# A two-layer trunk on one core: the sums of activation quarters made on POOL, and the matmuls that first write the sums' banks set behind the first product

## The chip, the core and the metric

The kernel runs on one core of a Trainium2 chip. The core's engines are TensorE (PE, with its weight loads PEld), VectorE (DVE), ScalarE (ACT), GpSimd (POOL) and SyncE (SP), which here only issues DMAs. The engines run side by side, each through its own list of instructions in order, and wait for each other through semaphores. The metric is the device time of one execution in microseconds (us).

## The reference

Two layers, each of three parts; every part has a normalisation before and after and is added to x.

```python
for l in range(DEPTH):
    h = hybrid_mixer(rmsnorm(x, pre_mix_g[l]), ...)
    x = x + rmsnorm(h, post_mix_g[l])
    h = memory_cross_attention(rmsnorm(x, pre_mem_g[l]), mem, ...)
    x = x + rmsnorm(h, post_mem_g[l])
    h = conv_ffn(rmsnorm(x, pre_ffn_g[l]), w_up[l], fconv_w[l], fconv_b[l], w_down[l])
    x = x + rmsnorm(h, post_ffn_g[l])

def conv_ffn(h, w_up, conv_w, conv_b, w_down):
    u = causal_dwconv(h @ w_up, conv_w, conv_b)
    a, g = jnp.split(u, 2, axis=-1)
    return (jax.nn.gelu(g, approximate=True) * a) @ w_down
```

x has 512 tokens of 1024 features; `w_up` is 1024 x 5632, that is 22 pairs of 128 linear and 128 gate columns. The change lies where the part `conv_ffn` of each layer begins.

## The kernel before

**Precision.** A float32 matrix product is made of three matmuls. `split` (L98) writes the rounded value of an operand on ACT (`ACT.copy`, L99: "hi") and the remainder on DVE (`DVE.tensor_sub`, L100: "lo"); `mm3` then adds hi x hi, hi x lo and lo x hi in one PSUM bank.

**Before the up projection.** After cross-attention the class `Tail` handles x in four pieces of 128 tokens, t = 0 to 3. For each piece `pre_norm` (L239) normalises, and `to_feature` (L270) transposes on PE, casts to hi on ACT (L276, tiles `B`), makes lo on DVE (L277, also `B`) and, for this part alone, copies the float32 values to a tile `T` (ACT, L279). With pieces t = 2 and t = 3 `Forms.add` (L299) makes sums and differences of the quarters of the activations (pieces 0 with 2, and 1 with 3), four additions of 128x512 (L308 to L311), each of which needs the one before it, and splits two results of 128x1024 into the tiles `S` (hi on ACT L99, lo on DVE L100): the first can be split after the second addition, the other after the fourth.

**The up projection.** Columns 0 and 1 are made in the plain way by `feat_halves`: four units (linear and gate of each), 24 matmuls of 256 tokens for the first half of each unit, then the same for the second half, which needs pieces 2 and 3. A unit's result is a PSUM bank `pg`; when it is complete, ACT takes the middle tap of the convolution (L1026), DVE the other two (L1031), and gate units then go through the gelu (L1053). From column 2 on, `up_products` makes seven smaller products per column in place of eight (Strassen's scheme in Winograd's form), from sums of weight quarters (POOL, L1101 to L1104, tiles `T`, numbers 1 to 4 of `add_up`) and the sums `S`. Each product is 12 matmuls of 256 tokens. Products 1, 5, 6 and 7 go to banks `pa`; products 2, 3 and 4 are added on top of sums that ACT and DVE have copied into two of four banks `pg` per column (`total(j)`). These four `pg` banks are those in which `feat_halves` made its four units, so each comes free when the taps of that unit are done. Before the first copy into them, in columns 2 and 3 alone, one matmul with `start=True` writes each of the two banks of a column; its values are overwritten.

**What sets the order.** PE's instructions stand in the order of the code, into which waiting tasks such as `pre_norm` are mixed by a clock of estimated times. Up to the end of `feat_halves` the instructions of ACT, DVE and POOL are ordered by the framework's scheduler, which places them by its own estimates; behind that point (`manual_schedule`, in `ffn`) they stand in the order of the code, and so do SP's DMAs within `up_products`. Weight tiles `raw` have two buffers and `rg` two: a load waits until the last reader of its buffer is done. `whi` and `wlo` have five.

The two steps of the prediction lie in `Forms.add` (L308 to L311) and in `first` (L1148). Layers are called 0 and 1, pieces t2 and t3; column 2's weights are tiles `whi`, `wlo` and `T`, column 3's the next ones.

Of the kernel before, what the change touches and what calls it, by code (L numbers as in the profile page):

```python
# [14 lines left out]
ALU = mybir.AluOpType  # L15
# [23 lines left out]
def trunk_kernel(ctx: ExitStack, tc: tile.TileContext, x4, memt, w, gw, gains, mcw, fcw, gb,  # L39
# [3 lines left out]
    ACT, DVE, POOL, PE, SP = nc.scalar, nc.vector, nc.gpsimd, nc.tensor, nc.sync  # L43
# [7 lines left out]
    def nm(s):  # L51
        uid[0] += 1
        return f"{s}_{uid[0]}"
# [4 lines left out]
    def pa():  # L58
        return ps.tile([128, 512], F32, tag="a", name=nm("pa"), bufs=4)
# [38 lines left out]
    def split(src, hi, lo):  # L98
        ACT.copy(hi, src)  # L99
        DVE.tensor_sub(lo, src, hi.bitcast(F32))  # L100
# [3 lines left out]
    def mm(o, lhs, rhs, **kw):  # L104
        n = math.prod(o.shape[1:])
        now[0] += 0.0025 + (max(0.218, n / 600) if rhs.dtype == F32 else max(0.107, n / 2400))
        PE.matmul(o, lhs, rhs, **kw)  # L107
# [5 lines left out]
    def mm3(o, lh, ll, rh, rl, start, stop, **kw):  # L113
        mm(o, lh, rh, start=start, stop=False, **kw)
        mm(o, lh, rl, start=False, stop=False, **kw)
        mm(o, ll, rh, start=False, stop=stop, **kw)
# [164 lines left out]
    class Forms:  # L281
# [19 lines left out]
        def add(self, t, xf):  # L301
            self.xf[t] = xf
            if t < 2:
                return
            self.s = self.s or [self.wide(F32R) for _ in range(4)]
            a, b = self.xf[t - 2], xf
            a11, a12, a21, a22 = a[:, :4], a[:, 4:], b[:, :4], b[:, 4:]
            DVE.tensor_add(a22, a21, a22)  # L308
            DVE.tensor_sub(a21, a11, a21)
            DVE.tensor_sub(a11, a22, a11)  # L310
            DVE.tensor_sub(a12, a12, a11)  # L311
            c = slice(128 * (t - 2), 128 * (t - 2) + 128)
            for i, f in ((0, b), (2, a)):
                split(f, self.s[i][:, :, c], self.s[i + 1][:, :, c])
# [755 lines left out]
    def up_products(l, fp, xn, forms, us, conv_first, conv_rest, gated, gtiles):  # L1070
# [13 lines left out]
        raws, rgs, ts, ws, e1s, p5s = {}, {}, {}, {}, {}, {}  # L1084
# [48 lines left out]
        def total(j):  # L1133
            i = 2 * (j % 2)
            return sums[i], sums[i + 1]

        def product(o, j, i, start=False):
            kind, c0 = {1: ("a", 0), 2: ("a", 512), 5: ("t", 0), 6: ("t", 512), 3: ("b", 0), 7: ("u", 0),
                        4: ("u", 512)}[i]
            hi, lo = ws[j, kind]  # L1140
            for q in range(4):
                c = slice(c0 + 128 * q, c0 + 128 * q + 128)
                rh, rl = act[i](q)
                mm3(o, hi[:, c], lo[:, c], rh, rl, start and q == 0, q == 3, skip_group_check=not start)
                if q % 2:
                    yield

        def first(j):  # L1148
            e1s[j] = pa()[:, left]
            if j < j0 + 2:  # L1150
                for o in total(j):
                    mm(o, ws[j, "a"][0][:, :128], xn[0][:, 0, :], start=True, stop=True)
            yield from product(e1s[j], j, 1, True)

        for j in (j0, j0 + 1):
            load_a(j)
# [3 lines left out]
        for kind in "atu":  # L1160
            high(j0, kind)
            low(j0, kind)
        high(j0, "b")
        yield from first(j0)
        ACT.copy(total(j0)[0][:, left], e1s[j0])
        high(j0 + 1, "a")
        low(j0 + 1, "a")
        ready = []
        for j in range(j0, NF + 1):
# [31 lines left out]
            if j + 1 == NF:  # L1201
                ready.append(down_tile(0))
            else:
                yield from first(j + 1)
# [168 lines left out]
```

## Time and profile before

| | us |
|---|---|
| median of 3 runs | 1577.7 |
| lowest and highest of them | 1573.72, 1581.47 |
| profiled execution | 1576.06 |
| its span, first to last instruction | 1574.3 |

| engine | busy us | share of the span |
|---|---|---|
| PE | 1547.4 | 98% |
| DVE | 1049.2 | 67% |
| ACT | 892.0 | 57% |
| POOL | 326.5 | 21% |

The profile gives each instruction's start and length on its engine, and in brackets the idle time of the engine before it with the instruction that ended it. An instruction that is held up after it was sent shows a longer time, not idle time. A line with x2 or more merges instructions of one kind that follow each other. The granted clock of PE is 0.997 of full speed over the span.

### The profile page before, as it was taken

What the parts mean: (1) busy time and instruction counts of PE and PEld (TensorE: products, weight loads), DVE (VectorE), ACT (ScalarE), POOL (GpSimd) and SP (SyncE); (2) the same over time, 40 slices, a digit from 0 to 9 for tenths busy, and PEclk for the clock granted to TensorE, in tenths of its full rate; (3) what the DMA queues carried; (4) which work ended last, traced back from release to release, by engine and by line L of the source; (5) the groups of instructions that cost most, each with busy time, mean ns of one, the idle gap of its engine ahead of it and who ended that gap; (6) DMA issues with size and microseconds to landing.
All of it is one profiled execution on the core that took longest, in us unless ns stands there. A gap on an engine that the chain in (4) does not pass through costs nothing.

```text
span 1574.3 us, 24497 instructions
## 1 busy us (share of the span) xinstructions
PE 1547.4 (98%) x9480; PEld 1371.0 (87%) x9480; DVE 1049.2 (67%) x1808; ACT 892.0 (57%) x1578; POOL 326.5 (21%) x292
## 2 busy tenths in 40 slices
PE   7999999999999999999999999999999999999998
PEld 5788888998899999988887888889888899999886
DVE  5687646746597777763376886557566977777433
ACT  5677574545466666653257775745445666666321
POOL 0000110100026666600010002101000466663000
PEclk9999999999999999999999999999999999999999
DMA  5421244552242333332333223445411233332331
GB/s 177 129 94 62 92 137 153 155 187 94 68 136 95 108 108 108 108 121 94 108 95 107 94 74 94 137 144 161 161 54 42 96 108 108 108 114 82 127 102 58
DMA packets 55430, 173.13 MB, mean 110 GB/s; under 512 B 6801, under 2 KB 9617, under 8 KB 55314
## 3 DMA queue, kind: packets, MB, share of 16 engines
q1 hardware_dynamic: 55314, 171.57, 33.4%
q8 instruction: 74, 1.21, 0.3%
q14 instruction: 42, 0.34, 0.1%
HBM read 165.22 MB, written 6.33 MB: 109 GB/s over the span
## 4 chain that ended last, share of the span: by engine, by line
PE 82%; DVE 6%; DMA 5%; ACT 3%; issue 2%; POOL 1%; SPq 0%; POOLq 0%; DVEq 0%; ACTq 0%
PE pg L107 51%; PE pa L107 28%; PE pa L111 2%; DMA raw<-in_w_dram 2%; DVE wlo L100 1%; DMA raw<-in_memt_dram 1%; ACT whi L99 1%; DVE xg L256 1%; POOL sm L230 1%; ACT junk L235 1%; DVE x L369 1%; DMA raw<-dk 1%; DVE wlo L1126 1%; DMA raw<-dv 1%; DMA dk<-kf 0%
## 5 line engine op out<-in xcount | busy, mean ns | idle before, releaser
L107 PE MATMUL pg<-B,whi 128*128 128x256 f32 (+1 forms) x1800 | 420.7, 327 | 8.2 <-DVE ql L995 3.9
L100 DVE TENSOR_TENSOR wlo<-raw,whi 128x1024 fp32r<-128x1024 f32 x188 | 230.6, 1228 | 215.7 <-ACT whi L99 213.1
L99 ACT CAST whi<-raw 128x1024 fp32r<-128x1024 f32 x188 | 197.2, 1050 | 217.8 <-PE pg L107 139.7
L107 PEld LDWEIGHTS pg<-B,whi 128*128 128x128 f32 x1800 | 290.8, 189 | 28.3 <-DVE ql L995 4.3
L107 PE MATMUL pg<-whi,B 128*128 128x512 f32 x896 | 297.8, 399 | 0.0
L107 PE MATMUL pg<-B,wlo 128*128 128x256 f32 (+1 forms) x896 | 288.4, 322 | 0.0
L107 PEld LDWEIGHTS pg<-whi,B 128*128 128x128 f32 x896 | 168.6, 188 | 35.1 <-DVE B L100 1.3
L230 POOL TENSOR_TENSOR sm<-sm,mhalf 128x1 f32<-128x1 f32 x56 | 34.3, 612 | 724.2 <-DVE sm L355 548.3
L107 PEld LDWEIGHTS pg<-B,wlo 128*128 128x128 f32 x896 | 168.9, 188 | 13.6
L107 PE MATMUL pg<-wlo,B 128*128 128x512 f32 x448 | 175.3, 391 | 0.6 <-DVE sm L248 0.6
L107 PE MATMUL pa<-S,whi 128*128 128x256 f32 x960 | 175.5, 283 | 0.0
L1031 DVE SCALAR_TENSOR_TENSOR u<-pg,fcw,u 128x511 f32<-128x511 f32 (+1 forms) x176 | 131.3, 747 | 38.2 <-ACT u L1026 35.2
L107 PEld LDWEIGHTS pa<-S,whi 128*128 128x128 f32 x960 | 148.4, 190 | 0.0
L107 PE MATMUL pa<-S,wlo 128*128 128x256 f32 x480 | 135.6, 282 | 0.0
L1126 DVE TENSOR_TENSOR wlo<-T,whi 128x1024 fp32r<-128x1024 f32 x80 | 103.9, 1299 | 9.7 <-ACT whi L1120 9.7
L107 PE MATMUL pa<-whi,S 128*128 128x512 f32 x320 | 105.9, 390 | 0.0
L107 PE MATMUL pg<-whi,S 128*128 128x512 f32 x320 | 105.4, 390 | 0.0
L1120 ACT CAST whi<-T 128x1024 fp32r<-128x1024 f32 x80 | 83.5, 1044 | 32.9 <-PE pg L107 30.8
L1026 ACT ACTIVATE u<-pg,fcw 128x512 f32<-128x512 f32 x88 | 68.5, 779 | 57.2 <-PE pg L107 37.2
L107 PEld LDWEIGHTS pg<-wlo,B 128*128 128x128 f32 x448 | 84.7, 189 | 15.8 <-DVE wlo L100 1.0
L107 PEld LDWEIGHTS pa<-S,wlo 128*128 128x128 f32 x480 | 90.9, 189 | 0.0
L1126 POOL TENSOR_TENSOR b<-rg,b 128x512 fp32r<-128x512 f32 x40 | 51.6, 1290 | 142.7 <-ACT b L1120 142.7
(264 smaller groups left out, 2942.5 us busy)
## 6 DMA issues: line engine op xcount, KB each, us to landing
raw<-in_w_dram SPq DMA_DIRECT2D x228, 512.0 KB, 3.5
rg<-in_w_dram SPq DMA_DIRECT2D x40, 512.0 KB, 3.5
gain<-in_gains_dram SPq DMA_DIRECT2D x11, 512.0 KB, 4.0
raw<-in_memt_dram SPq DMA_DIRECT2D x20, 256.0 KB, 3.0
tb<-tb_d SPq DMA_DIRECT2D x16, 256.0 KB, 3.5
x<-in_x_dram SPq DMA_DIRECT2D x8, 256.0 KB, 5.6
e<-nmu_d SPq DMA_DIRECT2D x8, 256.0 KB, 3.7
dv<-vf SPq DMA_DIRECT2D x8, 256.0 KB, 4.4
```

Of the source, the lines that this page charges most:

```text
L99: ACT.copy(hi, src)
L100: DVE.tensor_sub(lo, src, hi.bitcast(F32))
L107: PE.matmul(o, lhs, rhs, **kw)
L111: PE.transpose(o, src, idn)
L230: POOL.tensor_tensor(r, v, mhalf[:, :1], ALU.pow)
L235: ACT.activation(junk[:, :src.shape[-1]], src, AF.Square, accum_out=s_)
L256: DVE.scalar_tensor_tensor(xg, xt[:, c], r, g[h], ALU.mult, ALU.mult)
L369: DVE.scalar_tensor_tensor(xs[t][:, cc], self.hg[hh, t], r, xs[t][:, cc], ALU.mult, ALU.add)
L1026: ACT.activation(u, acc, AF.Identity, bias=fcw_t[:, m, 3:4], scale=fcw_t[:, m, 2:3])
L1031: DVE.scalar_tensor_tensor(u[:, q:], acc[:, :512 - q], fcw_t[:, m, 2 - q:3 - q], u[:, q:], ALU.mult, ALU.add)
L1120: ACT.copy(ws[j, kind][0], source(j, kind))
L1126: sub(ws[j, kind][1], source(j, kind), ws[j, kind][0].bitcast(F32), ALU.subtract)
```

## The change

The four additions of `Forms.add` move from DVE to POOL, with the same operands. In `first` the one or two matmuls that write the banks of a column's sums for the first time are issued behind the twelve matmuls of product 1 in place of ahead of them.

```diff
             a11, a12, a21, a22 = a[:, :4], a[:, 4:], b[:, :4], b[:, 4:]
-            DVE.tensor_add(a22, a21, a22)
-            DVE.tensor_sub(a21, a11, a21)
-            DVE.tensor_sub(a11, a22, a11)
-            DVE.tensor_sub(a12, a12, a11)
+            POOL.tensor_tensor(a22, a21, a22, ALU.add)
+            POOL.tensor_tensor(a21, a11, a21, ALU.subtract)
+            POOL.tensor_tensor(a11, a22, a11, ALU.subtract)
+            POOL.tensor_tensor(a12, a12, a11, ALU.subtract)
...
         def first(j):
             e1s[j] = pa()[:, left]
+            yield from product(e1s[j], j, 1, True)
             if j < j0 + 2:
                 for o in total(j):
                     mm(o, ws[j, "a"][0][:, :128], xn[0][:, 0, :], start=True, stop=True)
-            yield from product(e1s[j], j, 1, True)
```

Because the scheduler orders ACT, DVE and POOL here, the move of four additions also changes the order of other instructions. On ACT in layer 0, between the end of piece t2 and column 2's first weights (`B`: hi of piece t3; `S_4656`: the split that needs t2's fourth addition; `whi_4695`: hi of the fourth unit of `feat_halves`; `whi_4956`: column 2's):

```order
 L420 COPY kf_4645<-pg_4620 128x256
 L276 CAST B_4157<-pa_4667 128x4x128
+L99 CAST S_4656<-T_4403 128x8x128
+L99 CAST whi_4695<-raw_4693 128x1024
+L279 COPY T_4666<-pa_4667 128x512
 L276 CAST B_4158<-pa_4709 128x4x128
-L99 CAST whi_4695<-raw_4693 128x1024
-L99 CAST S_4656<-T_4403 128x8x128
-L279 COPY T_4666<-pa_4667 128x512
 L1120 CAST whi_4956<-raw_4940 128x1024
 L279 COPY T_4666<-pa_4709 128x512
```

The cast that needs the fourth addition now stands ahead of the cast of the fourth unit's weights, which stood ahead of it before.

On ACT in layer 1, at the same place (`S_12568` and `S_12570`: the two splits of t2; `B_12168` and `B_12169`: hi of piece t3):

```order
 L279 COPY T_12539<-pa_12540 128x512
 L279 COPY T_12539<-pa_12554 128x512
+L99 CAST S_12568<-T_12539 128x8x128
+L99 CAST S_12570<-T_12372 128x8x128
 L276 CAST B_12168<-pa_12617 128x4x128
-L99 CAST S_12568<-T_12539 128x8x128
 L276 CAST B_12169<-pa_12631 128x4x128
-L99 CAST S_12570<-T_12372 128x8x128
 L279 COPY T_12616<-pa_12617 128x512
 L279 COPY T_12616<-pa_12631 128x512
```

Both splits of t2 now stand ahead of both casts of piece t3; before, one cast stood ahead of each split.

On POOL in layer 0 (`T_4563`, `T_4403`: t2's operands; `T_4666`, `T_4491`: t3's; `T_4948`, `T_4949`: column 2's weight sums):

```order
 L230 TENSOR_TENSOR sm_4453<-sm_4451,mhalf 128x1
+L308 TENSOR_TENSOR T_4563<-T_4563 128x512
+L309 TENSOR_TENSOR T_4563<-T_4403,T_4563 128x512
+L310 TENSOR_TENSOR T_4403<-T_4563,T_4403 128x512
+L311 TENSOR_TENSOR T_4403<-T_4403 128x512
+L308 TENSOR_TENSOR T_4666<-T_4666 128x512
 L1101 TENSOR_TENSOR T_4948<-rg_4942,raw_4940 128x512
+L309 TENSOR_TENSOR T_4666<-T_4491,T_4666 128x512
 L1102 TENSOR_TENSOR T_4948<-rg_4942,T_4948 128x512
+L310 TENSOR_TENSOR T_4491<-T_4666,T_4491 128x512
+L311 TENSOR_TENSOR T_4491<-T_4491 128x512
 L1103 TENSOR_TENSOR T_4949<-rg_4942 128x512
```

The additions of t3 and those of column 2's weights now share one list, two of the latter between the former. In layer 1 the list is L1101, L1102, the four additions of t3, L1103, L1104.

## Rows read from the trace of the kernel before

**Rows 1.** The page's part 1: busy us, share of the span, instructions.

```profile
PE 1547.4 (98%) x9480; PEld 1371.0 (87%) x9480; DVE 1049.2 (67%) x1808; ACT 892.0 (57%) x1578; POOL 326.5 (21%) x292
```

**Rows 2.** Waits of PE, whole span: us in total, times, longest us.

```profile
PE pg L107 <- DVE u L1031: 2.8, 2, 2.0
PE pa L107 <- DVE wlo L1126: 2.2, 2, 1.2
```

**Rows 3.** Timeline of DVE, layer 0: start us, length us, then the instruction.

```profile
452.93 1.22 DVE L100 TENSOR_TENSOR wlo<-raw,whi 128x1024 fp32r<-128x1024 f32 x1 [1.00 <-ACT whi L99]
...
455.79 1.22 DVE L100 TENSOR_TENSOR wlo<-raw,whi 128x1024 fp32r<-128x1024 f32 x1 [0.31 <-ACT whi L99]
...
459.87 1.21 DVE L100 TENSOR_TENSOR wlo<-raw,whi 128x1024 fp32r<-128x1024 f32 x1
...
464.87 1.79 DVE L308 TENSOR_TENSOR T<-T 128x512 f32<-128x512 f32 x1
...
476.83 2.97 DVE L1031 SCALAR_TENSOR_TENSOR u<-pg,fcw,u 128x511 f32<-128x511 f32 x4
```

**Rows 4.** Timeline of ACT, layer 0.

```profile
452.79 0.59 ACT L279 COPY T<-pa 128x512 f32<-128x512 f32 x1
...
457.93 1.05 ACT L99 CAST whi<-raw 128x1024 fp32r<-128x1024 f32 x1
459.39 1.05 ACT L99 CAST S<-T 128x1024 fp32r<-128x1024 f32 x1 [0.41 <-DVE T L311]
...
462.86 0.59 ACT L279 COPY T<-pa 128x512 f32<-128x512 f32 x1 [0.99 <-DVE B L277]
...
470.77 0.78 ACT L1026 ACTIVATE u<-pg,fcw 128x512 f32<-128x512 f32 x1
```

**Rows 5.** Timeline of POOL, layer 0.

```profile
462.56 1.30 POOL L1101 TENSOR_TENSOR T<-rg,raw 128x512 f32<-128x512 f32 x1 [14.41 <-DMA rg<-in_w_dram]
463.94 2.17 POOL L1102 TENSOR_TENSOR T<-rg,T 128x512 f32<-128x512 f32 x1
```

**Rows 6.** Timeline of PE, layer 0.

```profile
477.27 0.40 PE L107 MATMUL pg<-B,whi 128*128 128x512 f32 x1
...
478.51 0.48 PE L107 MATMUL pg<-B,whi 128*128 128x512 f32 x1 [0.84 <-DVE u L1031]
...
478.82 0.40 PE L107 MATMUL pa<-B,whi 128*128 128x256 f32 x2
...
480.24 0.40 PE L107 MATMUL pa<-S,whi 128*128 128x256 f32 x2
...
483.09 0.62 PE L107 MATMUL pg<-B,whi 128*128 128x512 f32 x2
...
483.56 0.40 PE L107 MATMUL pa<-B,whi 128*128 128x256 f32 x2
...
484.94 0.39 PE L107 MATMUL pa<-B,wlo 128*128 128x256 f32 x1 [0.99 <-DVE wlo L1126]
```

**Rows 7.** Timeline of ACT, layer 1.

```profile
1223.57 1.07 ACT L279 COPY T<-pa 128x512 f32<-128x512 f32 x2
1225.35 0.59 ACT L276 CAST B<-pa 128x512 fp32r<-128x512 f32 x1 [0.70 <-PE pa L111]
...
1235.63 0.78 ACT L1026 ACTIVATE u<-pg,fcw 128x512 f32<-128x512 f32 x1
```

**Rows 8.** Timeline of PE, layer 1.

```profile
1228.79 0.40 PE L107 MATMUL pg<-B,whi 128*128 128x256 f32 x2
...
1243.95 0.47 PE L107 MATMUL pg<-B,whi 128*128 128x512 f32 x1 [1.98 <-DVE u L1031]
...
1252.40 0.39 PE L107 MATMUL pa<-B,wlo 128*128 128x256 f32 x1 [1.25 <-DVE wlo L1126]
```

**Rows 9.** Windows, all engines: from:to, us, busy us by engine, PEclk, DMA share, GB/s.

```profile
453.00:462.00 9.00, 9.00 (x79) 9.00 (x78) 8.65 (x10) 7.40 (x11) 0.00 (x0) 1.00 0.76 259
...
1245.20:1248.60 3.40, 3.40 (x19) 3.40 (x18) 3.40 (x3) 2.76 (x5) 3.32 (x3) 0.50 0.47 154
```

## The prediction

> **What bounds the kernel now.** I read the busy shares first: PE is busy 98% of the span [rows 1], so the time is PE's work plus what PE waits. The list of PE's waits comes next: of the places that this change touches, the taps of the convolution (DVE, L1031) cost 2.8 us and the remainder of column 3's weights (`wlo`, L1126) 2.2 us, each once per layer [rows 2]. So no more than some 5 us can be won here, 0.3%. The timelines of each engine around these waits show what lies ahead of them: DVE is busy 8.65 of 9 us [rows 9], and ACT holds a short list in which each instruction waits for DVE, PE or a load. The question is whether POOL makes the sums early enough for what now stands behind them.
>
> **What the additions cost on either engine.** DVE loses 16 additions of some 0.7 us (16 x 0.7 = 11 us over both layers, some of it lengthened, as the 1.79 us of [rows 3]). On POOL an instruction of this shape takes 1.30 us, and one that needs its result starts 1.38 us after it (462.56 to 463.94 [rows 5]). So a chain of four takes 5.5 us in place of 2.8. To that come meetings: POOL's L1102 took 2.17 us and DVE's L308 1.79 us at the same time [rows 3, 5], the one starting its work when the other has ended. I take it that a POOL addition and a DVE instruction with two inputs in SBUF follow each other, at 1.2 us for a POOL addition and 1.1 for 1024 elements on DVE (1.22 less the overlap with the next), while DVE instructions with an input in PSUM (L277, L1031) go on beside. The bounds are a meeting that costs nothing and this; the rows lie near the second.
>
> The Trainium skill, "Perfetto Trace Analysis", section "Optimizing Scalar/DVE Operations", says that work may be offloaded to Scalar or GPSIMD if DVE is saturated, and warns that GPSIMD and DVE share a read port, so that it might not help between those two. By its first half the change should gain, which is the second rival below; by its second half it should not, and the lengthened rows above speak for that half.
>
> **Layer 0, piece t2.** I set the instructions one behind the other in the new order, with the lengths of the rows. The last copy of t2 ends at 453.38 (452.79 + 0.59 [rows 4]). POOL's first addition waits for DVE's `wlo` (452.93 + 1.22 [rows 3]) and runs 454.15 to 455.4, the second to 456.7. DVE's next `wlo`, ready at 455.79 [rows 3], waits for it and runs to 457.8; the third addition follows to 459.05; DVE's first `S` remainder then to 460.1; the fourth addition ends at 461.3. Before, the cast that waits for it started at 459.39 [rows 4]. That alone would hurt nobody, but on ACT the cast of the fourth unit's weights now stands behind this cast: it runs 462.3 to 463.35 in place of 457.93 [rows 4], and DVE's remainder of it, behind that of `S`, ends at 464.8, where it started at 459.87 [rows 3]. PE reaches that unit five units of 24 matmuls ahead of 477.27 [rows 6]; 12 matmuls take 1.42 us (478.82 to 480.24 [rows 6]), so at 463.1, and needs the remainder in its third matmul. **PE stands 1.6 us** where it did not stand before.
>
> **Layer 0, piece t3.** The second copy of t3, at 462.86 before [rows 4], waits on ACT and for DVE's L277 until 465.4. POOL then holds the four additions with two of column 2's weight sums between them: first addition 466.6 to 467.8 (behind a DVE remainder), L1101 to 469.0, second to 470.2, L1102 to 471.4, third to 473.8 (one meeting with `S`), fourth to 475.1. ACT's casts of `S` (475.2) and of column 2's weights stand ahead of the first unit's middle tap, which so starts at 477.1 in place of 470.77 [rows 4]. DVE follows: `S` to 477.5, column 2's remainder to 479.8 (meeting L1104), taps of unit 1 to 481.3, the next remainder to 483.4 (meeting POOL), taps of unit 2 to 484.9. Before, the latter ended at 478.35 (two of the four in the row at 476.83 [rows 3]).
>
> PE leaves `feat_halves` at 477.27 + 1.6 = 478.9, makes product 1 (1.42 us) and wants the two banks at 480.3. They come free at 481.3 and 484.9. So the matmuls that moved behind product 1 wait still longer than before (0.84 us [rows 6]). Behind them products 5 and 6 and the first two matmuls of column 3's product 1 run until PE waits for column 3's remainder, as before. That one hangs on DVE: before, it took 6.6 us from the taps of unit 2 (478.35) to the waiting matmul at 484.94 [rows 6]; of these about 1 us was a meeting with L1104, which POOL now has behind it, so 484.9 + 5.5 = 490.4. Then the two bank matmuls of column 3 are still to do, 0.47 us (483.09 to 483.56 [rows 6]), which before were done ahead of the wait. **Layer 0: 490.4 + 0.47 - 484.94 = +5.9 us.**
>
> **Layer 1.** The copy of t2 ends at 1224.64 [rows 7]; the four additions, with two meetings, end at 1226.0, 1228.4, 1229.7 and 1232.0. Both casts of `S` stand ahead of those of t3's `B`: the second ends at 1233.1, and `B` hi, at 1225.35 before for its first half [rows 7], comes at 1233.6, `B` lo at 1235.0. PE wants both at 1228.79 for the second halves [rows 8]: **it stands about 6 us** in two waits. The copies of t3 end at 1236.2, the four additions, behind L1101 and L1102, run 1237.0 to 1243.2, and the first middle tap starts at 1244.2 in place of 1235.63 [rows 7]. From there DVE makes remainders and taps without a gap, the second bank is free at 1251.2 (PE had it at 1243.95 [rows 8]), and column 3's remainder, about 6.5 us later, at 1257.7 (1252.40 before [rows 8]). PE's 6 us are no cost of their own: they lie ahead of this later wait, which sets the end. **Layer 1: 1257.7 + 0.47 - 1252.40 = +5.8 us.**
>
> The same walk along the old order gives 484.8 and 1252.8 for the two matmuls that the rows have at 484.94 and 1252.40, so I trust it to half a microsecond per layer.
>
> **The moved matmuls by themselves.** In both layers column 3's remainder is a wait behind them that hangs on DVE, not on PE. What PE gains by not waiting for a bank it waits there, and the two matmuls of column 3 come behind that wait: +0.47 us per layer, already in the sums above. The cover is that wait; without it up to 1.42 us per layer of bank waits would be hidden.
>
> **What costs nothing.** SP's loads wait for later readers (column 3's `raw` for the fourth unit's remainder, 3.7 us later), but its cast is itself some 6 us later. POOL's b remainders and column 3's sums come later by 4 us and are read later by 6. Past column 3 nothing on DVE or ACT is closer to PE than before, so nothing of the loss is won back.
>
> **Sum.** 5.9 + 5.8 = 11.7 us on the profiled execution's 1576.06, 1587.8. The median of the three runs is 1.6 us above that execution, so I forecast 1577.7 + 11.7 = 1589.
>
> **Rivals.** 1. *The additions meet nothing on the way*: each takes 1.30 us whatever DVE does. Then t2's chain ends 1.4 to 2 us earlier and t3's likewise, and the same walk gives +1.9 and +2.4: 1582. For it: L1101 was not lengthened [rows 5]. Against it: L1102 right behind it was, by 0.87 us, and DVE's L308 by 1.1 [rows 3]. 2. *Faster: DVE is what the banks wait for*. Freed of four additions per piece it finishes the taps earlier, and both bank waits and the waits for `wlo` go: -5 us [rows 2], 1573. It decides if POOL's chain is no longer than DVE's was: t2's took 6.0 us from the copy to the cast behind the fourth addition (453.38 to 459.39 [rows 4]); POOL's takes 5.5 unhindered and 7.9 by my walk, and for t3 column 2's sums stand in the same list. 3. *The clock falls on top.* After the 1.98 us wait of layer 1 [rows 8] the granted clock was 0.50, that is 1.2 in place of 2.4 GHz, for 3.4 us [rows 9], in which PE does half the work: 1.7 us. The new waits are longer, so a fall in each layer is likely; most of it would lie ahead of the last wait and vanish in it, but one that begins behind it costs 1.7 us per layer: 1589.4 + 3.4 = 1593. 4. *It does nothing that shows*: the casts that overtook are ready anyway, 1578.
>
> **Chances.** Forecast 0.72 (own range 1584 to 1594), clock falls behind the last wait 0.13, no meetings 0.09, faster 0.03, nothing 0.03. The range takes in the falls and stops just above the middle of the no-meetings case: 1583 to 1595. About 0.5%, 7.9 us, is what can be told from no change here: slower by more 0.80 (the forecast's most part and the falls), within it 0.17, faster 0.03.
>
> **What would show it.** In the new profile PE should wait near 463.3 to 464.8 for a cast and a remainder (L99, L100), near 481 to 485 for L1031, and in layer 1 from 1228.8 to 1235 for L276 and L277 (layer 1's times shifted by layer 0's loss); POOL's L308 to L311 should show lengths up to 2.3 us beside DVE's L100 and L1126, and the first middle tap of each layer should start 6 to 9 us later. If PE's waits at L276 are under 3 us, the first rival holds; if the `wlo` of column 3 arrives within 3 us of before, my account of DVE's list is wrong.

## The result, and the profile after

| | before | changed |
|---|---|---|
| median, us | 1575.58 (6 runs) | 1587.92 (6 runs) |
| lowest and highest | 1573.72, 1581.47 | 1584.73, 1590.51 |
| profiled execution, its span | 1576.06, 1574.3 | 1587.3, 1585.5 |

The ratio of changed to before is 1.0071, with a 95% interval of 1.0057 to 1.0084: about 11 us slower. The forecast was 1589.0, with a range of 1583 to 1595.

I compare traces by stretches with fixed ends, since elsewhere in the span the profiled executions differ by up to some 3 us whatever the edit. In each layer the **stretch** runs from the start of ACT's second copy of piece t2 (L279) to its third copy L1173. These are both ends for layer 0, from ACT's timeline of the changed kernel (start us, length us, instruction):

```profile
451.73 0.59 ACT L279 COPY T<-pa 128x512 f32<-128x512 f32 x1
...
515.73 0.36 ACT L1173 COPY pg<-pa 128x256 f32<-128x256 f32 x1 [0.80 <-PE pa L107]
```

Before, the first stands at 452.79 [rows 4] and the third L1173 at 510.65. So layer 0 took 64.00 us in place of 57.86, **+6.15**; layer 1, measured in the same way, 59.15 in place of 54.05, **+5.09**. The rest of the span differs by less than 0.1 us in sum. In this execution layer 0's stretch begins 1.06 us earlier than before and layer 1's 6.15 us later; a time "on the clock of before" is shifted by so much.

PE's waits over the whole span of the changed kernel, with those that [rows 2] has (L1031 2.8 us, L1126 2.2 us):

```profile
PE pg L107 <- DVE u L1031: 5.4, 3, 3.1
PE pg L107 <- ACT B L276: 4.7, 1, 4.7
...
PE pa L107 <- DVE wlo L1126: 1.5, 1, 1.5
PE pa L107 <- ACT pg L1165: 1.0, 1, 1.0
PE pg L107 <- DVE wlo L100: 0.9, 1, 0.9
...
PE pg L107 <- DVE B L277: 0.8, 1, 0.8
```

The waits for the fourth unit (L100), for t3's hi (L276) and for ACT's copy of product 1 (L1165) are new; that for t3's lo (L277) grew from 0.41 us, and the one for the taps (L1031) became longer. DVE's busy time went from 1049.2 us [rows 1] to 1036.3, and POOL's from 326.5 to 350.1; PE's share stayed at 98%. DVE had less to do, and the kernel became slower.

POOL in layer 0, the four additions of t2, then those of t3 with two of column 2's weight sums between them (what [rows 5] shows of before is L1101 and L1102 here):

```profile
452.40 1.83 POOL L308 TENSOR_TENSOR T<-T 128x512 f32<-128x512 f32 x1 [5.32 <-ACT T L279]
454.31 1.29 POOL L309 TENSOR_TENSOR T<-T,T 128x512 f32<-128x512 f32 x1
455.68 2.15 POOL L310 TENSOR_TENSOR T<-T,T 128x512 f32<-128x512 f32 x1
457.91 2.15 POOL L311 TENSOR_TENSOR T<-T 128x512 f32<-128x512 f32 x1
464.84 1.58 POOL L308 TENSOR_TENSOR T<-T 128x512 f32<-128x512 f32 x1 [4.78 <-ACT T L279]
466.38 1.31 POOL L1101 TENSOR_TENSOR T<-rg,raw 128x512 f32<-128x512 f32 x1
467.65 1.29 POOL L309 TENSOR_TENSOR T<-T,T 128x512 f32<-128x512 f32 x1
468.89 1.30 POOL L1102 TENSOR_TENSOR T<-rg,T 128x512 f32<-128x512 f32 x1
470.15 2.27 POOL L310 TENSOR_TENSOR T<-T,T 128x512 f32<-128x512 f32 x1
472.50 1.28 POOL L311 TENSOR_TENSOR T<-T 128x512 f32<-128x512 f32 x1
```

Of the eight additions three took 1.28 or 1.29 us and three 2.15 or 2.27; the long ones lie beside a DVE instruction with two inputs in SBUF (L100). From the last copy of t2 to the cast behind the fourth addition it takes 7.8 us (452.32 to 460.09), where it took 6.0 on DVE. The Trainium skill, "Perfetto Trace Analysis", section "Optimizing Scalar/DVE Operations", says that work may be handed from a saturated DVE to GPSIMD, but that the two share an SBUF read port, so it might not help; these rows, in which the same addition takes 1.28 us alone and up to 2.27 beside DVE, agree with its warning.

ACT then shows what waits for the chains, in layer 0:

```profile
460.09 1.05 ACT L99 CAST S<-T 128x1024 fp32r<-128x1024 f32 x1 [2.65 <-POOL T L311]
461.04 1.04 ACT L99 CAST whi<-raw 128x1024 fp32r<-128x1024 f32 x1
...
473.81 1.05 ACT L99 CAST S<-T 128x1024 fp32r<-128x1024 f32 x1 [3.79 <-POOL T L311]
474.76 1.04 ACT L1120 CAST whi<-T 128x1024 fp32r<-128x1024 f32 x1
475.71 0.77 ACT L1026 ACTIVATE u<-pg,fcw 128x512 f32<-128x512 f32 x1
```

The first middle tap starts at 475.71, which is 476.77 on the clock of before, where it stood at 470.77 [rows 4]: 6.0 us late. ACT in layer 1, where the second of t2's casts is followed by t3's hi, and the first tap comes later:

```profile
1237.72 1.04 ACT L99 CAST S<-T 128x1024 fp32r<-128x1024 f32 x1 [2.51 <-POOL T L311]
1238.67 1.07 ACT L276 CAST B<-pa 128x512 fp32r<-128x512 f32 x2
...
1249.95 0.77 ACT L1026 ACTIVATE u<-pg,fcw 128x512 f32<-128x512 f32 x1
```

PE, in layer 0 and then in layer 1:

```profile
463.59 0.39 PE L107 MATMUL pg<-B,wlo 128*128 128x256 f32 x1 [0.94 <-DVE wlo L100]
...
479.96 0.47 PE L107 MATMUL pg<-B,whi 128*128 128x512 f32 x1 [0.68 <-DVE u L1031]
483.57 0.76 PE L107 MATMUL pg<-B,whi 128*128 128x512 f32 x1 [3.14 <-DVE u L1031]
...
489.68 0.28 PE L107 MATMUL pa<-B,wlo 128*128 128x256 f32 x1
...
1239.30 0.58 PE L107 MATMUL pg<-B,whi 128*128 128x256 f32 x1 [4.70 <-ACT B L276]
...
1256.92 0.47 PE L107 MATMUL pg<-B,whi 128*128 128x512 f32 x1 [1.59 <-DVE u L1031]
...
1263.18 0.39 PE L107 MATMUL pa<-B,wlo 128*128 128x256 f32 x1 [1.48 <-DVE wlo L1126]
```

These answer to [rows 6] and [rows 8]. In layer 1 the stretch ends, as before, with the wait for column 3's remainder. In layer 0 there is no such wait any more: the matmul that had it starts at 489.68, and the remainder was ready at 488.88, from DVE's timeline:

```profile
487.66 1.22 DVE L1126 TENSOR_TENSOR wlo<-raw,whi 128x1024 fp32r<-128x1024 f32 x1
```

The window behind the 3.14-us wait shows why PE came late (from:to, us, busy us of PE, PEld, DVE, ACT, POOL, then the granted clock):

```profile
482.90:489.60 6.70, 6.03 (x27) 5.97 (x28) 5.96 (x9) 5.58 (x9) 4.47 (x4) 0.50 0.12 48
```

The granted clock was 0.50, 1.2 GHz in place of 2.4, for 6.83 us from 482.8 on; I call such a piece a half clock. Layer 1 has one of 6.83 us as well, from 1237.2 on, around PE's early waits. Before, the only half clock within the two stretches was the 3.41 us of [rows 9].

### The profile page after: what moved, and what is told of

Same layout as the page of the kernel before. It is cut to its first block, busy times and chain, and to the rows that moved or that the text cites. A ratio compares the mean times of both kernels' runs of the same rounds, so it can differ in the third digit from the quotient of the medians.

```text
span 1585.5 us, 24494 instructions
## 1 busy us (share of the span) xinstructions
PE 1550.0 (98%) x9480; PEld 1373.3 (87%) x9480; DVE 1036.3 (65%) x1792; ACT 892.0 (56%) x1578; POOL 350.1 (22%) x308
## 4 chain that ended last, share of the span: by engine, by line
PE 81%; DVE 5%; DMA 5%; ACT 3%; POOL 3%; issue 2%; SPq 0%; POOLq 0%; DVEq 0%; ACTq 0%
PE pg L107 50%; PE pa L107 29%; PE pa L111 3%; DMA raw<-in_w_dram 2%; DVE wlo L100 1%; DMA raw<-in_memt_dram 1%; DVE xg L256 1%; ACT whi L99 1%; ACT junk L235 1%; POOL sm L230 1%; DVE x L369 1%; DMA raw<-dv 1%; DMA raw<-dk 1%; DVE wlo L1126 0%; POOL T L311 0%
## 5 line engine op out<-in xcount | busy, mean ns | idle before, releaser
L100 DVE TENSOR_TENSOR wlo<-raw,whi 128x1024 fp32r<-128x1024 f32 x188 | 231.8, 1234 | 216.1 <-ACT whi L99 215.7
L1031 DVE SCALAR_TENSOR_TENSOR u<-pg,fcw,u 128x511 f32<-128x511 f32 (+1 forms) x176 | 131.4, 747 | 37.9 <-ACT u L1026 34.9
L1126 DVE TENSOR_TENSOR wlo<-T,whi 128x1024 fp32r<-128x1024 f32 x80 | 104.0, 1300 | 10.1 <-ACT whi L1120 10.1
L1126 POOL TENSOR_TENSOR b<-rg,b 128x512 fp32r<-128x512 f32 x40 | 51.7, 1293 | 145.5 <-ACT b L1120 145.5
```

The costliest lines, as they stand in the source:

```text
L1031: DVE.scalar_tensor_tensor(u[:, q:], acc[:, :512 - q], fcw_t[:, m, 2 - q:3 - q], u[:, q:], ALU.mult, ALU.add)
L1126: sub(ws[j, kind][1], source(j, kind), ws[j, kind][0].bitcast(F32), ALU.subtract)
```

## The experiments

Each run was timed beside the kernel before on the same chip. "In the stretches" gives the length of layer 0's stretch and then of layer 1's, in the one profiled execution of each run, against before's 57.86 and 54.05 us.

**1. The additions alone**, without the moved matmuls.

> The additions on POOL alone; the matmuls that first write the banks stay ahead of product 1. My theory: the loss is POOL's chain, so nearly all of the 12 us stays, +5.6 us in layer 0 and +4.9 us in layer 1, +10.6 against the kernel before; only the 0.47 us per layer of the two matmuls of column 3 goes. PE's waits near the end of the plain columns: L1031 twice per layer, of some 2.6 and 3.6 us in layer 0 and 2.5 and 2.6 us in layer 1, and L276 about 4.8 us in layer 1. Rival, the moved matmuls make half of the loss because they put PE's bank waits behind the first product: about +6.

Measured: ratio 1.0073 (1.0049 to 1.0097); in the stretches +6.24 and +5.12. PE waited 2.10 and 3.15 us for the two banks in layer 0, 0.54 and 2.11 in layer 1 (2.5 and 2.6 were expected there), and never for L1126. So the additions are the loss, and the matmuls add nothing to it in sum: 6.15 - 6.24 and 5.09 - 5.12 are -0.1 and 0.0 us, not 0.47 per layer. That is a balance of unlike things. With the matmuls moved, PE's waits at the banks of layer 0 are 3.82 us in place of 5.25, but the half clock there lasts 6.83 us in place of 3.41; in layer 1 a half clock of 3.41 us behind the last wait is gone (from 1258.6 on in this run), and PE's waits from the banks on are 4.04 us in place of 2.65.

**2. The moved matmuls alone.**

```diff
             e1s[j] = pa()[:, left]
+            yield from product(e1s[j], j, 1, True)
             if j < j0 + 2:
...
-            yield from product(e1s[j], j, 1, True)
```

> The moved matmuls alone; the additions stay on DVE. My theory: what PE gains by not waiting for a bank it waits for column 3's remainder (L1126), and the two matmuls of column 3 come behind that wait, +0.45 us per layer, +0.9 in all; PE's waits for L1126 grow from 2.2 to about 4.5 us in all, those for L1031 shrink. Rival, the bank waits are hidden behind the first product and that is won: -0.8 us in layer 0 and -1.4 in layer 1, -2.2.

Measured: ratio 1.0017 (1.0005 to 1.0030), in the stretches +0.71 and +1.45. PE's waits over the span:

```profile
PE pa L107 <- DVE wlo L1126: 5.1, 2, 3.4
```

The last one in PE's timeline of layer 1:

```profile
1251.19 0.58 PE L107 MATMUL pa<-B,wlo 128*128 128x256 f32 x1 [3.37 <-DVE wlo L1126]
```

The 2.2 us at L1126 [rows 2] became 5.1, and those at L1031 fell from 2.8 to 0.9: the gain at the banks is waited out at the remainder, as forecast. In layer 0 the waiting matmul starts at the same time as before (0.01 us earlier, counted from the stretch's start), so that the 0.71 us arise behind it: 0.47 are the two matmuls, and 0.22 two columns that each took 0.11 us longer (last section). In layer 1 it starts 0.48 us earlier than before and the stretch ends 1.45 later, so 1.9 us arise behind it. There a half clock of 3.41 us begins at this last wait (1251.1), where before it lay ahead of it [rows 9]: half of 3.41 and the two matmuls would be 2.2. This is a sum, and no run shows the half clock apart.

**3. The additions on the first 8 tokens only.** What is left out is the rest of the sums.

```diff
-            POOL.tensor_tensor(a22, a21, a22, ALU.add)
+            POOL.tensor_tensor(a22[:, :, :8], a21[:, :, :8], a22[:, :, :8], ALU.add)
...
```

> The additions on POOL on the first 8 of 128 tokens alone (the rest of the sums is left out), the matmuls as before. ACT's order in layer 1 is the one of the changed kernel in the first part: both splits of t2 ahead of both casts of t3. My theory, the length of POOL's chain is the loss: it is gone, and with DVE freed of 16 additions of 0.7 us the kernel is some 5 us faster than before (-2 in layer 0, -3 in layer 1), PE's wait for L276 in layer 1 is under 1 us. Rival, ACT's order is the loss: layer 1 keeps its +5 us and PE's wait for L276, so about +3 in all. Rival, freeing DVE wins nothing here: 0.

Measured: ratio 0.9959 (0.9942 to 0.9976), in the stretches -2.17 and -2.37. No wait is left in layer 0, and in layer 1 the early one is 1.18 us, for L277, none for L276. ACT's order there is the changed kernel's as far as t3's copies and does no harm with short additions. So in layer 1 it is the time until the sums are there, not the order by itself; in layer 0 the order of this run is another, and run 4 answers for it.

**4. ACT's order tied to the one before, in one point.** The split that needs the fourth addition is put behind t3's casts and the cast of the fourth unit's weights by a tie that only orders ACT's list; the additions are on POOL as in run 1.

```diff
+            if t == 3:
+                split(self.xf[0], self.s[2][:, :, :128], self.s[3][:, :, :128]); behind(casts[-1], units4[-1], feats[-1])
...
-            for i, f in ((0, b), (2, a)):
+            for i, f in ((0, b), (2, a))[:t - 1]:
```

> The additions on POOL at full length, the matmuls as before, and ACT's order tied to the one before in one point: the split of t2 that needs the fourth addition stands behind both casts of t3 and the cast of the fourth unit's weights. My theory: PE's wait for the fourth unit (L99, L100) in layer 0 goes and its waits for L276 and L277 in layer 1 shrink from 6 to under 3 us, but the end of each layer's stretch still hangs on POOL's chain of t3 and the remainder of column 3: +3.3 us in layer 0 and +4.6 in layer 1, about +8. Rival, the order is the whole loss: within 1 us of before. Rival, the order is without effect, because only the last wait counts: +10.6, as with the additions alone.

Measured: ratio 1.0047 (1.0029 to 1.0066); in the stretches +2.77 and, in the profiled execution, +6.53.

PE's timeline, layer 0 and then layer 1:

```profile
481.15 0.76 PE L107 MATMUL pg<-B,whi 128*128 128x512 f32 x1 [3.02 <-DVE u L1031]
...
1233.13 0.38 PE L107 MATMUL pg<-B,whi 128*128 128x256 f32 x1 [0.90 <-ACT B L276]
1234.60 0.39 PE L107 MATMUL pg<-B,whi 128*128 128x256 f32 x1 [1.09 <-DVE B L277]
1251.27 0.47 PE L107 MATMUL pg<-B,whi 128*128 128x512 f32 x1 [3.62 <-ACT u L1026]
1253.85 0.77 PE L107 MATMUL pg<-B,whi 128*128 128x512 f32 x1 [2.11 <-DVE u L1031]
```

The wait for the fourth unit is gone, and those for t3's hi and lo shrank from 5.5 to 2.0 us. In layer 0 the order is 6.24 - 2.77 = 3.5 us of the additions' loss, more than the 2.3 that I had put on it. In layer 1 the early waits went and the loss did not: PE waits about as long later, for the taps, as the prediction's sentence on layer 1 has it. The 6.53 is not typical: this execution took 1587.2 us, the other five 1582.1 to 1584.2. It has a half clock of 6.83 us from 1252.4 on, around the last wait, and longer columns in layer 1 (last section; 0.22 us of the stretch, 2 us of the layer). By the ratio the whole loss is about 7.4 us; less layer 0's 2.77 that leaves some 4.6 for layer 1, an estimate, as expected.

**5 and 6. One piece at a time**: POOL adds for t2 alone, then for t3 alone.

```diff
-            DVE.tensor_add(a22, a21, a22)
+            E = POOL if t == 2 else DVE; E.tensor_tensor(a22, a21, a22, ALU.add)
...
```

> Only piece t2's additions on POOL, t3's on DVE, the matmuls as before. From the second copy of t2 to the third L1173 copy of each layer I expect, worked out with the lengths of the traces, +2.5 us in layer 0 (PE's wait for the fourth unit's weights, L99 and L100, and a later chain of taps) and +4.5 us in layer 1 (PE's wait for L276 of about 4.7 us, after which DVE and ACT have the same work still to do), +7 in all. Rival, only t3's additions count because they are the last before the waits: within 1 us of before. Rival, the two pieces add up to the loss of both, +11.4 in these stretches, half each: +5.7.

> Only piece t3's additions on POOL, t2's on DVE, the matmuls as before. In the same stretches: +2.6 us in layer 0 and +3.5 in layer 1, +6 in all, from PE's waits for the taps (L1031) alone; PE waits neither for the fourth unit's weights nor for L276. Together with t2 alone this is more than the loss of both in layer 1, since both end in the same list of DVE. Rival, only t3's additions count: +11.4, as with all of them. Rival, half each: +5.7, which this run alone can't tell from my theory.

Measured: t2 alone 1.0054 (1.0034 to 1.0075), +2.65 and +4.97 in the stretches; t3 alone 1.0058 (1.0041 to 1.0075), +5.10 and +4.18. Each piece loses by itself, and in neither layer do the two add up (7.75 against 6.24 us for both in layer 0, 9.15 against 5.12 in layer 1). Of the 2.65 us 0.22 are again longer columns. t2 came out as worked out, but t3 in layer 0 was 2.5 us worse. Its trace has a half clock of 6.83 us there, in the windows of that run (columns as above):

```profile
480.90:487.70 6.80, 4.83 (x22) 4.77 (x22) 5.57 (x9) 4.05 (x6) 5.76 (x4) 0.50 0.24 77
```

**7. Filling the waits.** To keep the clock up, 12 and 24 matmuls whose result nobody reads were put ahead of the two bank matmuls of column 2.

```diff
-            e1s[j] = pa()[:, left]
+            p = pa(); e1s[j] = p[:, left]
...
+                    for _ in range(n): PE.matmul(p[:, right], ws[j, "a"][0][:, :128], xn[0][:, 0, :256], start=True, stop=True)
                     mm(o, ws[j, "a"][0][:, :128], xn[0][:, 0, :], start=True, stop=True)
```

> The kernel with t3's additions alone on POOL, and besides 12 matmuls of 128x256 ahead of the first and 24 ahead of the second bank matmul of column 2 in each layer, written to a half of product 1's bank that nobody reads; they take 1.4 and 2.9 us and lie in PE's waits of 1.69 and 3.13 us (layer 0) and 2.63 and 5.15 us (layer 1). If the half clock behind these waits is what made layer 0 lose 5.10 us where 2.6 were worked out without it, the granted clock stays at 2.4 GHz there and layer 0 loses 2.6 to 3 us, layer 1 some 3.5 in place of 4.18. Rival, the fall costs nothing because PE would wait anyway: layer 0 stays at +5.1.

> The changed kernel, with 4 and 24 such matmuls ahead of the two bank matmuls of column 2 in layer 0, in waits of 0.68 and 3.14 us. My theory: the half clock of 6.83 us there only took the place of a wait for column 3's remainder, which was ready 0.6 us before PE came to it; so the clock stays at 2.4 GHz, PE waits some 2.5 us at L1126 in its place, and layer 0 loses 5.5 us in place of 6.15. Rival, the half clock is a loss of its own: layer 0 loses about 3 us, 3.4 less.

Both were inconclusive: 1.0065 (1.0047 to 1.0084) and 1.0080 (1.0065 to 1.0096), in the stretches +6.16 and +7.18, and +8.84 and +6.25. With the extra matmuls the scheduler put the fourth unit's gelu ahead of ACT's copy of product 1 in layer 0, so a new wait came up, here in PE's timeline of the first of the two:

```profile
486.89 0.79 PE L107 MATMUL pa<-S,whi 128*128 128x256 f32 x2 [1.96 <-ACT pg L1165]
```

In the second that wait is 3.38 us; besides, the extra matmuls follow product 1 in its bank there, and the values that come out are no longer the kernel's. For the kernel with t3 alone I tied ACT's and DVE's order, in these two points, to that of run 6 and filled once more:

```diff
-        low(j0 + 1, "a")
+        low(j0 + 1, "a"); behind(gelus[-1], casts[j0 + 1, "a"]); behind(muls[1], lows[j0 + 1, "a"])
```

> The kernel with t3's additions alone on POOL and the same 12 and 24 extra matmuls as in the run before it that had them, but with ACT's and DVE's order tied to the one without them (the gelu of the fourth unit behind the cast of column 3's first weights, and its product behind their remainder), which the scheduler had turned round there. The clock's theory: the granted clock stays at 2.4 GHz behind the waits, layer 0 loses 2.6 to 3 us in place of 5.10 and layer 1 about 3.5 in place of 4.18; PE waits at L1126 for column 3's remainder, which it did not before. Rival, the fall only took the place of a wait: 5.1 and 4.2 as before, and the wait is as much longer.

Measured: 1.0029 (1.0015 to 1.0042), in the stretches +2.57 and +4.13. The same window:

```profile
480.90:487.70 6.80, 6.80 (x59) 6.76 (x58) 6.10 (x9) 4.16 (x6) 6.01 (x4) 1.00 0.23 77
```

The extra matmuls, in PE's timeline of layer 0:

```profile
478.61 1.59 PE L1151 MATMUL pa<-B,whi 128*128 128x256 f32 x12
480.27 3.01 PE L1151 MATMUL pa<-B,whi 128*128 128x256 f32 x24
```

The clock stayed at 2.4 GHz in layer 0 and 2.5 us of the 5.10 were gone, as much as the sum without a fall had left unexplained. In layer 1 waits of 1.22 and 2.51 us were left beside the extra matmuls, and a half clock of 3.41 us in place of 10.24; the loss stayed. The wait at L1126 that I expected did not come.

**8. A candidate on the other side**: the kernel before, with the split of column 2's weight sums u, which product 7 alone needs, behind that of column 3's first weights; then with 22 extra matmuls in layer 1's wait, and last with the orders tied too.

```diff
-        for kind in "atu":
+        for kind in "at":
...
         low(j0 + 1, "a")
+        high(j0, "u"); low(j0, "u")
```

> The kernel before with one change of its own: the split of the weight sums u of column 2, which product 7 alone reads, stands behind the split of column 3's first weights and no longer ahead of the taps. If DVE's list ahead of the taps and of column 3's remainder is what PE waits for, as the explanation of the change needs, this takes one instruction of 1.2 us out of it: -1.8 us in layer 0 and -1.3 in layer 1, about -3, and PE's waits for L1126 go in layer 0 and shrink in layer 1. If the waits hang on something else (ACT's casts, the loads), no difference; if product 7 is then late, +2 to +3.

> The kernel with the split of u behind column 3's first weights, and 22 such matmuls ahead of the second bank matmul of column 2 in layer 1, where PE waits 2.97 us, the last wait of that stretch, with a half clock of 3.41 us behind it. If a fall behind the last wait costs what PE does less in it, layer 1 goes from -1.16 to about -2.9 us and the kernel is about 4.7 us faster than before. Rival, the fall is without effect: -3, as without the matmuls.

> The kernel with the split of u behind column 3's first weights, 22 extra matmuls ahead of the second bank matmul of column 2 in layer 1, and the orders of ACT and DVE tied in the same way. If a fall behind the last wait costs what PE does less in it, layer 1 goes from -1.16 us (with the split of u moved alone) to about -2.5, and the kernel is 4 to 5 us faster than before. Rival, the fall is without effect: -3, as without the matmuls.

Measured: 0.9990 (0.9978 to 1.0001), not clear of no change by itself, in the stretches -1.84 and -1.16, a sum of -3.0 as worked out; with extra matmuls 0.9997 (0.9988 to 1.0006), -2.19 and +2.63, a wait of 2.7 us for ACT's copy of product 1 (L1164 there) as in run 7; with the orders tied 0.9977 (0.9962 to 0.9991), -1.71 and -1.57. The last is the fastest full version here, 1573.3 us, and beats both kernels. The first shows again that DVE's list ahead of the taps and remainders is what PE waits for: with one instruction less in it PE's waits in layer 0 fell from 1.83 us to 0.22. My expectation for the last missed in layer 1: the half clock behind the 2.97-us wait had cost 0.4 us (-1.16 became -1.57), not the 1.3 that would have made it -2.5, and without it PE waited 0.17 us at a bank and 0.33 at the remainder.

## Why the prediction was right, and where not

**The chains of layer 0 were right to 0.3 us.** On the clock of before: t2's fourth addition, worked out to end at 461.3, ended at 461.12; t3's, at 475.1, at 474.84; the banks, at 481.3 and 484.9, came at 481.02 and 484.63. PE's wait for the fourth unit was 0.94 us for 1.6. The meetings on which this rested are in POOL's rows, and rival 1, no meetings, falls with them and with PE's 4.70 us at L276, which it needed under 3.

**The end of layer 0 was right in size and wrong in kind.** The prediction had PE wait for column 3's remainder until 490.4, +5.9. The remainder was ready at 489.94 (488.88 + 1.06), but PE, at half clock, came only 0.8 us later, +6.15; that the two errors cancel is luck. The step that failed is the one that gave the clock's fall behind the last wait 13 in 100 and 1.7 us on top: a fall came there, 6.83 us long, mostly in the place of the wait that I had put there. By the window's row it took some 3 us from PE (6.03 busy at half clock), of which the remainder would have taken 2.2 anyway; an estimate, since DVE's and ACT's rows show no wait for PE between the taps of unit 2 and this remainder. No run shows it, because the one that filled this wait changed ACT's order (run 7). With t3 alone a fall of the same length cost 2.5 us. There product 1 stands behind the banks, so at half clock it came late too, and with it ACT's copy, which waited 0.84 us for it, and column 3's remainder, which waited 0.54 for ACT.

**Layer 1 was right in kind and 0.7 us too large.** Its times came 0.4 to 0.7 us earlier than worked out: second cast of S at 1231.57 in place of 1232.0, the bank at 1250.77 in place of 1251.2, the remainder's matmul at 1257.03 in place of 1257.7. PE's early wait was 5.5 us for "about 6", and, as forecast, was no cost of its own; the half clock around it lay ahead of the later waits too.

**The moved matmuls: the term held, the comparison without them did not.** In the changed kernel layer 1's waiting matmul comes 4.63 us later than before and the stretch ends 5.09 later; the 0.46 between them are the two matmuls behind the wait, as in layer 0 of run 2. Yet against the additions alone the moved matmuls cost nothing. The prediction took it that the stretch ends with the wait for column 3's remainder whether they are moved or not. With the additions on POOL and the matmuls left in place it ends otherwise: PE waits longest at the banks, runs 3.41 us at half clock behind them, and finds the remainder ready.

**The other rivals.** Freeing DVE does gain here, 4.5 us in the stretches when the additions are cut to 8 of 128 tokens (run 3), about the 5 us of the faster rival, but not when POOL's chain takes longer than DVE's. "Nothing that shows" fell: every version with POOL's additions at full length was slower.

**The sum.** 6.15 + 5.09 = 11.2 us for 11.7. The forecast's start was high: the median of before is 1575.58 with six runs and was 1577.7 with the three that were shown. The medians of six lie 12.3 us apart, 1.1 more than the stretches, which is within the spread of the runs. So 1587.9 came nearer to 1589.0 than its parts deserve.

## What to carry to other kernels

Moving work from a busy engine to an idle one pays only if the chain that somebody waits for gets shorter; compare the chain's length on either engine, with the meetings on the way, not the busy shares. Where a scheduler orders an engine's list, look at what else it turned round, since 3.5 us of layer 0 were the order here. A wait that disappears from the list of waits may have become a half clock, so read the granted clock of the window behind the wait before it.

## What the runs showed of the hardware

**The half clock came in pieces of 3.41, 6.83 and 10.24 us** within the stretches, each beside waits of PE that add up to between 2 and 8 us. Where a run took one away its cost ran from next to nothing (layer 1 with t3 alone, 10.24 us shortened to 3.41: 0.05 us) over 0.4 us (3.41 us, run 8) to 2.5 us (6.83 us, layer 0 with t3 alone).

**A column of products has two lengths.** In the experiment with the moved matmuls alone, ACT's copies L1173 follow each other by 10.08 us through all of layer 0 and by 9.97 through layer 1, with the granted clock at full and the same 84 matmuls per column:

```profile
550.31 0.36 ACT L1173 COPY pg<-pa 128x256 f32<-128x256 f32 x1 [0.82 <-PE pa L107]
560.39 0.36 ACT L1173 COPY pg<-pa 128x256 f32<-128x256 f32 x1 [0.82 <-PE pa L107]
...
1318.70 0.36 ACT L1173 COPY pg<-pa 128x256 f32<-128x256 f32 x1 [0.79 <-PE pa L107]
1328.67 0.36 ACT L1173 COPY pg<-pa 128x256 f32<-128x256 f32 x1 [0.80 <-PE pa L107]
```

That is 0.1200 us per matmul against 0.1187, and 2 us per layer. It showed in one layer each of five of the thirteen executions profiled after that of the kernel before (runs 2, 4, the first of 5 and 6, the second of 7, the second of 8), with no relation to the edit that I can see. It may be part of the spread of before's runs (1571.8 to 1582.3), which no run shows. Its cause stays open; it is why the stretches above end at the third column, where they hold 0.22 us of it.
